# Cached keys turned by VectorE instead of TensorE, and stores of ScalarE's results issued from ScalarE's queue

## The chip, the cores and the metric

The kernel runs on one core of one Trainium2 chip. The core has a matrix engine (TensorE; PE in the profile, and PEld for its weight loads), three engines for elementwise work (VectorE = DVE, ScalarE = ACT, GpSimd = POOL), and SyncE (SP), which here does nothing but issue transfers. Sixteen transfer engines move data between the main memory and the on-chip memory. Each engine runs its own instructions in order; semaphores tell one engine that another has finished. The metric is the device time of one execution in microseconds, lower is better.

## What is computed

One step of a streaming encoder trunk for two groups of requests that share the weights: a prompt of 2048 tokens, and a sample of 8 sequences of 16 tokens, each with 1024 cached positions. All data is float32.

```python
h = rms_norm(x, norm_g[l])
(a_x, a_b, a_c, a_z, g_q, g_f, g_i, g_z,
 s_q, s_k, s_v, s_z, m_a, m_b, m_c) = split_cols(h @ w_in[l])
...
q = rms_norm(s_q.reshape(B, T, SB_HEADS, SB_DH), q_norm_g[l])
k = rms_norm(s_k.reshape(B, T, SB_HEADS, SB_DH), k_norm_g[l])
...
    k_all = jnp.concatenate([past_k.astype(k.dtype), k], axis=1)
    v_all = jnp.concatenate([past_v.astype(v.dtype), v], axis=1)
    o_sb = sb_attend(q, k_all, v_all, P + jnp.arange(T), jnp.arange(P + T))
o_c = o_sb.reshape(B, T, W_SB).astype(x.dtype) * jax.nn.silu(s_z)
...
m = jax.nn.sigmoid(m_a) * y_a + jax.nn.sigmoid(m_b) * y_b + jax.nn.sigmoid(m_c) * y_c
return x + m @ w_out[l], conv_new, S_new.astype(x.dtype), k, v
```

There are three branches: a gated convolution (A), a gated recurrence with a matrix state (B) and stick-breaking attention with 8 heads of 64 (C). In C the weight of a key is a sigmoid of its score times the product of one minus the sigmoids of all later keys. The sample's queries meet the 1024 cached keys of their sequence (`cache_k`, 8 x 1024 x 8 x 64 floats, 16.8 MB) besides their own; the prompt has no cache. New keys and values are outputs as well, and the three branch outputs are merged by sigmoid gates computed from `h`.

## The kernel before

Tokens go in 17 tiles of 128: tile 0 is the whole sample (8 x 16), tiles 1 to 16 are the prompt. Three groups of 5, 6 and 6 tiles (`GROUPS`) are projected one after the other. A float32 product is made of three products of rounded parts (`PASS3`), so each weight is kept as a high and a low half. `run_jobs` goes through a list of jobs for a group: `chan_job` gives 128 output columns for all tokens of a chunk (`proj_chan`, L710), `tok_job` 256 columns for one token tile at a time (`proj_tok`, L721). In the first group the weights are loaded, split and stored in that form; in the next two they are loaded again (`wload`, L208 and L201).

What is done with each projection's result:

- `gate_job` (24 jobs in each group, two chunks each): ScalarE takes the sigmoid from PSUM into `gm`, and a store to the scratch tensor `GM` follows (L1176, L1177).
- `post_v`: ScalarE copies the values into `vf`; two stores go to the output and to the scratch tensor `VV` (L835 to L837).
- `post_qk`: queries and keys are normed, turned on TensorE into a PSUM tile of its own and stored.

Each projection yields its cost after every few matmuls, and `run_jobs` spends it, times a rate, on background work kept as Python generators: the recurrence `hbg`, and in `bg` the sample's attention (from group 1) and the prompt's attention (from group 2 on). The costs that the generators yield are written out by hand. The order in which an engine gets its instructions is fixed when the kernel is built, from this order and from the dependences; on the chip an engine doesn't leave it.

`sample_attention` is the part in question. It goes over 8 sequences in three segments each, of 2, 3 and 3 blocks of 128 cached positions, last positions first, 24 segments and 64 blocks in all. For a segment:

- `keys(m)` loads each block, 128 positions x 512 columns, into `kc` with one transfer (L455; three buffers, shared under the tag `cst`), turns it with four TensorE transposes into a PSUM tile `tp` (L458) and copies that with ScalarE into the segment's `kt` (L459; two buffers), which has the head dimension on partitions and the position along the row. PSUM tiles `tp` have two buffers, shared with all other transposes of the kernel.
- `scores(m)` multiplies with the queries (L476), takes two sigmoids on ScalarE, and the running product on VectorE (L489, L490).
- `turned(m)` turns the weights on TensorE (L499) and loads the cached values; `values(m)` multiplies them (L522).

After a sequence's third segment, ScalarE copies the output of that sequence into `od` (L527), 128 partitions (8 heads x 16 queries) x 128 columns. Of these columns a head uses only one half. Eight stores of 16 x 64 put the halves in use to `OCS` (L529), [128 queries, 512]. At the end `OCS` is loaded in one transfer (L548), turned on TensorE (L551) and gated.

After the last group, the merge (L1440) and the output projection (L1471) follow, with the rest of the prompt's attention as background. All transfers but the indirect gathers of the recurrence are issued by SyncE.

Of the kernel before, what the change touches and what calls it, by code (L numbers as in the profile page):

```python
# [8 lines left out]
F32 = mybir.dt.float32  # L9
# [7 lines left out]
P = 128  # L17
# [3 lines left out]
NB = 8  # L21
TS = 16
# [76 lines left out]
def trunk(ctx: ExitStack, tc: tile.TileContext, x_prompt, x_sample, cache_conv, state_hgrn, cache_k, cache_v,  # L99
# [3 lines left out]
    nc = tc.nc  # L103
# [6 lines left out]
    def rows(prompt, sample, t):  # L110
        return sample if t == 0 else prompt[(t - 1) * P:t * P]
# [9 lines left out]
    vp_rows = v_prompt[0, 0].rearrange("t h d -> t (h d)")  # L121
    vs_rows = v_sample[0].rearrange("b t h d -> (b t) (h d)")
# [6 lines left out]
    dram = ctx.enter_context(tc.tile_pool(name="dram", bufs=1, space=DRAM))  # L129
# [11 lines left out]
    def ps_tp(dt=F32):  # L141
        return pst[0].tile([P, 512], dt, tag="tp", name="tp")

    def ps_pv():
        return ps.tile([P, 512], F32, tag="pv", name="pv", bufs=1)
# [8 lines left out]
    VV = dram.tile([NTOK, 8, 64], F32, name="VV")  # L154
# [1 line left out]
    OX = dram.tile([3, 4, 2, P, NTOK], F32R, name="OX")  # L156
    SZ = dram.tile([4, P, NTOK], F32, name="SZ")
    GM = dram.tile([3, 8, P, NTOK], F32, name="GM")
    OCS = dram.tile([P, 512], F32, name="OCS")


    idf = const.tile([P, P], F32, name="idf")
# [226 lines left out]
    def sample_attention():  # L389

        sx = ExitStack()
        sa = sx.enter_context(tc.tile_pool(name="sa", bufs=2, side="right"))
# [19 lines left out]
        for e in range(2):  # L412
            r = slice(64 * e, 64 * e + 64)
# [31 lines left out]
        def blocks(m):  # L445
            return 2 if order[m][1] == 2 else 3

        def keys(m):

            b, sg = order[m]  # L450
            kt = sa.tile([P, 4, 384], F32, tag="kt", name="kt", bufs=2)
            for bi in range(blocks(m)):
                blk = 3 * sg + bi
                kc = sa.tile([P, 512], F32, tag="cst", name="kc", bufs=3)
                nc.sync.dma_start(kc, cache_k[0, b, blk * P:(blk + 1) * P].rearrange("t h d -> t (h d)"))  # L455
                tp = ps_tp()
                for h in range(4):
                    nc.tensor.transpose(tp[:, h * P:(h + 1) * P], kc[:, h * P:(h + 1) * P], idf)  # L458
                nc.scalar.copy(kt[:, :, bi * P:(bi + 1) * P], tp.rearrange("p (h t) -> p h t", h=4))  # L459
                yield 1.3  # L460
            held[m] = [kt]

# [50 lines left out]
        def values(m):  # L513
            b, sg = order[m]
            at_, vs = held[m][2:4]
            if sg == 2:
                pvs[b] = ps_pv()
            pv = pvs[b]
            for bi, vc in enumerate(vs):
                for h in range(4):  # L520
                    c = bi * P + 32 * h
                    nc.tensor.matmul(pv[32 * h:32 * h + 32, 0:P].rearrange("p (e d) -> p e d", e=2),  # L522
                                     at_[:, c:c + 32], vc[:, 2 * h:2 * h + 2],
                                     start=sg == 2 and bi == 0, stop=sg == 0 and bi == 2, skip_group_check=True)
            if sg == 0:
                od = sa.tile([P, P], F32, tag="od", name="od", bufs=1)
                nc.scalar.copy(od, pv[:, 0:P])  # L527
                for h in range(8):
                    nc.sync.dma_start(OCS[b * TS:(b + 1) * TS, h * 64:(h + 1) * 64],  # L529
                                      od[h * TS:(h + 1) * TS, 64 * (h % 2):64 * (h % 2) + 64])  # L530


        last = len(order) - 1
        yield from keys(0)
        scores(0, masked(0))
        yield 0.7
        for m in range(last + 1):
            if m < last:
                yield from keys(m + 1)
            turned(m)  # L540
            yield 2.0
            z = masked(m + 1) if m < last else None
            values(m)
            if z is not None:
                scores(m + 1, z)
            yield 2.2
        oc = sa.tile([P, 512], F32, tag="cst", name="oc", bufs=3)
        nc.sync.dma_start(oc, OCS)  # L548
        tp = ps_tp()
        for j in range(4):  # L550
            nc.tensor.transpose(tp[:, j * P:(j + 1) * P], oc[:, j * P:(j + 1) * P], idf)  # L551
# [184 lines left out]
    def cols(chunk):  # L736
        return slice(chunk[0] * P, (chunk[-1] + 1) * P)
# [95 lines left out]
    def post_v(acc, t, s):  # L833
        vf = qk.tile([P, 256], F32, tag="kn", name="vf", bufs=5)
        nc.scalar.copy(vf, acc[:, :256])  # L835
        nc.sync.dma_start(rows(vp_rows, vs_rows, t)[:, s * 256:(s + 1) * 256], vf)
        nc.sync.dma_start(VV[t * P:(t + 1) * P, 4 * s:4 * s + 4].rearrange("t h d -> t (h d)"), vf)  # L837

# [298 lines left out]
    def group_jobs(g):  # L1139
        base = GROUPS[g][0][0] * P  # L1140
        chunks = GROUPS[g]
# [8 lines left out]
        def chan_job(name, blk, post, done=None):  # L1150
            def compute(w, ci, hT):
                acc = yield from proj_chan(w, hT)
                post(ci, acc)
                if done and ci == len(chunks) - 1:
                    done()
            return (chan_w(name, blk), compute, 1.0)
# [10 lines left out]
        for s in range(2):  # L1167
            qkv.append(tok_job("sv", s, post_v))
# [3 lines left out]
        def gate_job(x, d):  # L1172
            def post(ci, acc):
                n = len(chunks[ci]) * P
                gm = cv.tile([P, 384], F32, tag="gm", name="gm", bufs=3)
                nc.scalar.activation(gm[:, :n], acc[:, :n], AF.Sigmoid)  # L1176
                nc.sync.dma_start(GM[x, d][:, cols(chunks[ci])], gm[:, :n])  # L1177
            return chan_job(("ma", "mb", "mc")[x], d, post)

        def sz_job(j):  # L1180
# [192 lines left out]
    for g in range(len(GROUPS)):  # L1373
        run_jobs(g, group_jobs(g))
        if g == 0:
            p0.close()
            next(splitting)
            bg.add(sample_attention())
        if g == 1:
            prep.chunk(0)  # L1380
            bg.drain()
            for _ in splitting:
                pass
            mwx.close()
            p01.close()
            open_attention()
            for qi in range(4):
                bg.add(attention(qi), key=qi)
# [143 lines left out]
```

## Time and profile before

| | us |
|---|---|
| median of 3 runs (2876.0 to 2877.55) | 2877.0 |
| the profiled execution: its time | 2876.11 |
| its span, first to last instruction | 2873.2 |
| transfers | 649.76 MB, 370475 packets, mean 226 GB/s |

A profile is one execution as the hardware recorded it. Its page has the busy time of each engine, the chain of work that ended last (followed back from the last instruction, at each step to what released it), and groups of instructions that share line, engine, operation and tile, with count, busy time, mean duration, and the idle time of the engine in front of them with what ended it. In a row such as `tp<-idf,kc`, the written tile is on the left and the read ones on the right. A timeline row has start, duration, engine, line and operation; rows of one kind that follow each other are merged and counted. A transfer shows as the time its issue took on the issuing engine's queue (SPq for SyncE's), the time to landing, and the packets it was cut into; a packet is one contiguous run, and the share is the sum of the packets' times over 16 engines. Times of PE are modelled at their ends, as matmuls are pipelined, so its distances from start to start say more than its durations.

### The profile page before, as it was taken

What the parts mean: (1) busy time and instruction counts of PE and PEld (TensorE: products, weight loads), DVE (VectorE), ACT (ScalarE), POOL (GpSimd) and SP (SyncE); (2) the same over time, 40 slices, a digit from 0 to 9 for tenths busy, and PEclk for the clock granted to TensorE, in tenths of its full rate; (3) what the DMA queues carried; (4) which work ended last, traced back from release to release, by engine and by line L of the source; (5) the groups of instructions that cost most, each with busy time, mean ns of one, the idle gap of its engine ahead of it and who ended that gap; (6) DMA issues with size and microseconds to landing.
All of it is one profiled execution on the core that took longest, in us unless ns stands there. A gap on an engine that the chain in (4) does not pass through costs nothing.

```text
span 2873.2 us, 51723 instructions
## 1 busy us (share of the span) xinstructions
PE 2853.0 (99%) x19479; PEld 2662.3 (93%) x19479; DVE 1546.5 (54%) x3304; ACT 1018.7 (35%) x2375; POOL 331.8 (12%) x802
## 2 busy tenths in 40 slices
PE   9999999999999999999999999999999999999999
PEld 9999999999999999999999999999998888787888
DVE  5454635641344442545434747557485876867743
ACT  4333222242233332213334444434444444544420
POOL 3110000111200000001323111111010011010100
PEclk9999999999999999999999999999999999999999
DMA  8887777777678887746766454544447877878876
GB/s 306 305 276 247 231 241 244 231 243 243 212 249 266 276 265 243 243 167 192 237 215 202 146 173 136 173 139 151 144 145 238 286 234 239 266 250 266 271 250 210
DMA packets 370475, 649.76 MB, mean 226 GB/s; under 512 B 33481, under 2 KB 246306, under 8 KB 339506
## 3 DMA queue, kind: packets, MB, share of 16 engines
q1 hardware_dynamic: 369458, 644.36, 68.2%
q8 instruction: 154, 2.52, 0.4%
q0 software_dynamic: 768, 2.10, 0.2%
q14 instruction: 95, 0.78, 0.1%
HBM read 447.06 MB, written 199.27 MB: 225 GB/s over the span
## 4 chain that ended last, share of the span: by engine, by line
PE 76%; DVE 2%; DMA 2%; issue 1%; ACT 0%; POOL 0%; SPq 0%; DVEq 0%; POOLq 0%; ACTq 0%
PE acc L710 33%; PE acc L721 10%; PE acc L1440 9%; PE acc L1471 6%; PE pv L359 4%; PE tp L310 4%; PE z L330 2%; PE z L329 2%; PE z L1039 1%; PE tp L458 1%; DMA gate<-GM 1%; PE pv L522 1%; PE z L476 0%; PE hg L1086 0%; PE hg L826 0%
## 5 line engine op out<-in xcount | busy, mean ns | idle before, releaser
L710 PE MATMUL acc<-hx,w 128*128 128x384 f32 (+1 forms) x6816 | 1251.8, 333 | 0.1
L710 PEld LDWEIGHTS acc<-hx,w 128*128 128x128 f32 x6816 | 1106.5, 188 | 21.9 <-issue 15.2
L721 PE MATMUL acc<-w,hx 128*128 128x256 f32 x2544 | 328.6, 284 | 1.8 <-DVE hx L176 0.9
L342 DVE TENSOR_TENSOR_SCAN pr<-snb,carry 128x513 f32<-128x513 f32 x192 | 246.5, 1284 | 153.3 <-ACT snb L333 151.7
L721 PEld LDWEIGHTS acc<-w,hx 128*128 128x128 f32 x2544 | 310.9, 188 | 5.0 <-DVE hx L176 1.7
L311 ACT COPY aT<-tp 128x512 f32<-128x512 f32 (+2 forms) x320 | 167.6, 524 | 375.2 <-PE tp L310 361.3
L710 PE MATMUL acc<-hx,wst 128*128 128x384 f32 x1248 | 247.2, 344 | 0.0
L1440 PE MATMUL acc<-o,w 128*128 128x512 f32 (+2 forms) x1080 | 234.7, 363 | 1.8 <-DMA o<-OX 1.8
L333 ACT ACTIVATE snb<-z 128x512 f32<-128x512 f32 (+2 forms) x320 | 172.4, 539 | 144.5 <-PE z L330 140.4
L710 PEld LDWEIGHTS acc<-hx,wst 128*128 128x128 f32 x1248 | 215.4, 188 | 6.4 <-issue 3.7
L1440 PEld LDWEIGHTS acc<-o,w 128*128 128x128 f32 x1080 | 185.1, 188 | 33.8 <-issue 5.3
L347 DVE TENSOR_TENSOR sp<-sp,pr 128x512 f32<-128x512 f32 (+2 forms) x320 | 195.3, 611 | 29.2 <-POOL sp L338 3.7
L342 DVE TENSOR_TENSOR_SCAN pr<-snb,one 128x129 f32<-128x129 f32 (+3 forms) x128 | 114.4, 894 | 123.9 <-POOL snb L338 123.6
L310 PE MATMUL tp<-idf,sp 128*128 128x128 f32 x1088 | 171.3, 273 | 2.5 <-ACT aT L311 1.5
L335 ACT ACTIVATE sp<-z 128x512 f32<-128x512 f32 (+2 forms) x320 | 171.5, 536 | 0.0
L1471 PE MATMUL acc<-w,mh 128*128 128x256 f32 x816 | 161.2, 285 | 1.0 <-DVE yt L1479 0.8
L1176 ACT ACTIVATE gm<-acc 128x384 f32<-128x384 f32 (+1 forms) x144 | 68.2, 474 | 230.4 <-PE acc L710 197.5
L310 PEld LDWEIGHTS tp<-idf,sp 128*128 128x128 f32 x1088 | 131.8, 141 | 19.3 <-issue 4.4
L176 DVE TENSOR_TENSOR w<-wst,w 128x1024 fp32r<-128x1024 f32 x72 | 88.1, 1223 | 110.7 <-ACT w L175 107.9
L1471 PEld LDWEIGHTS acc<-w,mh 128*128 128x128 f32 x816 | 131.0, 188 | 7.2 <-issue 4.2
L329 PE MATMUL z<-Kt,Q 128*128 128x512 f32 (+2 forms) x320 | 128.8, 403 | 0.3 <-ACT sp L335 0.2
L359 PE MATMUL pv<-aT,Vt 128*64 128x512 f32 (+3 forms) x640 | 128.1, 535 | 0.0
(299 smaller groups left out, 3570.1 us busy)
## 6 DMA issues: line engine op xcount, KB each, us to landing
w<-W SPq DMA_DIRECT2D x168, 1024.0 KB, 6.0
W<-w SPq DMA_DIRECT2D x72, 1024.0 KB, 5.0
wst<-W SPq DMA_DIRECT2D x112, 512.0 KB, 5.1
wst<-in_w_in_dram SPq DMA_DIRECT2D x72, 512.0 KB, 5.1
GM<-gm SPq DMA_DIRECT2D x120, 192.0 KB, 3.7
W<-mwp SPq DMA_DIRECT2D x40, 512.0 KB, 4.2
Kt<-KT SPq DMA_DIRECT2D x160, 128.0 KB, 3.1
o<-OX SPq DMA_DIRECT2D x72, 256.0 KB, 4.7
```

The source lines that it names most:

```text
L310: nc.tensor.transpose(tp[:, j * P:(j + 1) * P], sp[:, j * P:(j + 1) * P], idf)
L311: nc.scalar.copy(aT[:, e, 0:nb, i * P:(i + 1) * P], tp[:, :w].rearrange("p (b q) -> p b q", q=P))
L329: nc.tensor.matmul(z[:, :w], Q1[:, i * P:(i + 1) * P], Kt[:, :w], start=True, stop=False)
L333: nc.scalar.activation(sn[:, 512 - w:512], z[:, :w], AF.Sigmoid, scale=-0.125)
L335: nc.scalar.activation(sp[:, :w], z[:, :w], AF.Sigmoid, scale=0.125)
L342: nc.vector.tensor_tensor_scan(pr[:, 512 - w:513][:, ::-1], s_in, s_in, one if diag else carry[e][i], ALU.mult, ALU.bypass)
L347: nc.vector.tensor_tensor(sp[:, :w], sp[:, :w], pr[:, 513 - w:513], ALU.mult)
L359: nc.tensor.matmul(pv[64 * e:64 * e + 64, c0:n], Vt[:, j, e], aT[:, e, j, c0:n], start=first and j == 0, stop=last and j == nb - 1, skip_g ...
L710: nc.tensor.matmul(acc[:, :n], w[0][a][:, k], hT[b][:, k, :n], start=k == 0 and i == 0, stop=k == KB - 1 and i == 2)
L721: nc.tensor.matmul(acc[:, :256], hT[b][:, k, ti * P:(ti + 1) * P], w[k // 4][a][:, k % 4], start=k == 0 and i == 0, stop=k == KB - 1 and i ...
L1440: nc.tensor.matmul(acc[:, :n], w[0][a][:, k, dd * P:(dd + 1) * P], box[x][b][:, k, sl], start=k == 0 and i == 0, stop=k == 3 and i == 2)
L1471: nc.tensor.matmul(acc[:, :256], box["l" if b else "h"][:, k, ti * P:(ti + 1) * P], w[k // 4][a][:, k % 4], start=k == 0 and i == 0, stop= ...
```

## The change

Three things change.

1. Cached keys. A block is loaded by four transfers of 32 partitions each. Partition 32a + p holds, for each of the four pairs of heads and each of the four groups of 32 positions, the 32 columns 32a to 32a + 31 of position p of that group. One VectorE instruction then turns all 32 x 32 squares of the tile and writes `kt`. The four TensorE transposes, the PSUM tile and ScalarE's copy are gone; the cost that `keys` yields is the same.
2. The sample's output. `od` is stored whole, with one transfer from ScalarE's queue in place of eight from SyncE's; at the end eight transfers from SyncE's queue, one for each head, pick the halves in use.
3. The stores of gates (`GM`) and values (the output and `VV`) are issued on ScalarE's queue in place of SyncE's. ScalarE wrote the tiles that they store.

```diff
-    OCS = dram.tile([P, 512], F32, name="OCS")
+
+    OCS = dram.tile([NB, P, 2, 64], F32, name="OCS")
...
             for bi in range(blocks(m)):
                 blk = 3 * sg + bi
-                kc = sa.tile([P, 512], F32, tag="cst", name="kc", bufs=3)
-                nc.sync.dma_start(kc, cache_k[0, b, blk * P:(blk + 1) * P].rearrange("t h d -> t (h d)"))
-                tp = ps_tp()
-                for h in range(4):
-                    nc.tensor.transpose(tp[:, h * P:(h + 1) * P], kc[:, h * P:(h + 1) * P], idf)
-                nc.scalar.copy(kt[:, :, bi * P:(bi + 1) * P], tp.rearrange("p (h t) -> p h t", h=4))
+
+                kc = sa.tile([P, 4, 4, 32], F32, tag="cst", name="kc", bufs=3)
+                keys_ = cache_k[0, b, blk * P:(blk + 1) * P].rearrange("(c p) h d -> p c (h d)", p=32)
+                keys_ = keys_.rearrange("p c (h x) -> p h c x", x=P)
+                for a in range(4):
+                    nc.sync.dma_start(kc[32 * a:32 * a + 32], keys_[:, :, :, 32 * a:32 * a + 32])
+                nc.vector.transpose(kt[:, :, bi * P:(bi + 1) * P].rearrange("p h (c q) -> p h c q", q=32), kc)
                 yield 1.3
...
                 nc.scalar.copy(od, pv[:, 0:P])
-                for h in range(8):
-                    nc.sync.dma_start(OCS[b * TS:(b + 1) * TS, h * 64:(h + 1) * 64],
-                                      od[h * TS:(h + 1) * TS, 64 * (h % 2):64 * (h % 2) + 64])
+                nc.scalar.dma_start(OCS[b].rearrange("r e d -> r (e d)"), od)
...
         oc = sa.tile([P, 512], F32, tag="cst", name="oc", bufs=3)
-        nc.sync.dma_start(oc, OCS)
+        for h in range(8):
+            nc.sync.dma_start(oc[:, h * 64:(h + 1) * 64], OCS[:, h * TS:(h + 1) * TS, h % 2])
...
         nc.scalar.copy(vf, acc[:, :256])
-        nc.sync.dma_start(rows(vp_rows, vs_rows, t)[:, s * 256:(s + 1) * 256], vf)
-        nc.sync.dma_start(VV[t * P:(t + 1) * P, 4 * s:4 * s + 4].rearrange("t h d -> t (h d)"), vf)
+        nc.scalar.dma_start(rows(vp_rows, vs_rows, t)[:, s * 256:(s + 1) * 256], vf)
+        nc.scalar.dma_start(VV[t * P:(t + 1) * P, 4 * s:4 * s + 4].rearrange("t h d -> t (h d)"), vf)
...
                 nc.scalar.activation(gm[:, :n], acc[:, :n], AF.Sigmoid)
-                nc.sync.dma_start(GM[x, d][:, cols(chunks[ci])], gm[:, :n])
+                nc.scalar.dma_start(GM[x, d][:, cols(chunks[ci])], gm[:, :n])
```

## Prediction

> **What bounds the kernel now.** I read the page's busy times and the chain that ended last, then the busy time by stage.
>
> ```profile
> span 2873.2 us, 51723 instructions
> ...
> PE 2853.0 (99%) x19479; PEld 2662.3 (93%) x19479; DVE 1546.5 (54%) x3304; ACT 1018.7 (35%) x2375; POOL 331.8 (12%) x802
> ...
> PE 76%; DVE 2%; DMA 2%; issue 1%; ACT 0%; POOL 0%; SPq 0%; DVEq 0%; POOLq 0%; ACTq 0%
> ```
>
> ```profile
> core 0: us, PE busy (x) PEld busy (x) DVE busy (x) ACT busy (x) POOL busy (x), PEclk, DMA share, GB/s
> 0.00:200.00 200.00, 195.84 (x1486) 192.94 (x1487) 91.86 (x189) 79.56 (x164) 45.11 (x104) 1.00 0.88 299
> 590.00:1140.00 550.00, 549.24 (x4304) 530.05 (x4304) 203.62 (x518) 175.49 (x439) 46.56 (x83) 1.00 0.76 249
> 1340.00:2170.00 830.00, 826.73 (x5372) 775.22 (x5371) 478.97 (x1039) 331.74 (x832) 148.72 (x345) 1.00 0.53 169
> ```
>
> TensorE sets the pace: of 2873.2 us it is idle for 20.2, and the chain runs through it. From 590 to 1140, where the cached keys are turned, it is idle for 0.76 us (550.00 less 549.24), VectorE is at 37%, ScalarE at 32%, the transfer engines at 0.76. So TensorE work taken away there is worth its full time, until the next thing is late. The first 200 us show the kernel with fuller transfer engines (0.88): TensorE then lost 4.16 us of 200.
>
> **The keys on TensorE (removed).** The groups of instructions by line, with count, busy us and mean ns:
>
> ```profile
> L458 PE MATMUL tp<-idf,kc 128*128 128x128 f32 x256 | 38.5, 273 | 0.8 <-DVE hx L176 0.8
> ...
> L459 ACT COPY kt<-tp 128x512 f32<-128x512 f32 x64 | 37.5, 588 | 58.6 <-PE tp L458 58.3
> ```
>
> The 273 ns of one transpose contain overlap with its neighbours, so I take the distance in the timeline (start, duration, engine and line):
>
> ```profile
> 930.50 0.49 ACT L1176 ACTIVATE gm<-acc 128x384 f32<-128x384 f32 x1 [1.53 <-PE acc L710]
> ...
> 931.02 0.32 SPq L1177 DMA_DIRECT2D GM<-gm  x1
> 931.43 2.40 SPq L455 DMA_DIRECT2D kc<-in_cache_k_dram  x3
> ...
> 944.14 0.54 PEld L458 LDWEIGHTS tp<-idf,kc 128*128 128x128 f32 x4
> ...
> 946.69 0.53 PEld L458 LDWEIGHTS tp<-idf,kc 128*128 128x128 f32 x4
> ...
> 947.18 3.11 PEld L710 LDWEIGHTS acc<-hx,w 128*128 128x128 f32 x18
> ...
> 950.28 0.53 PEld L458 LDWEIGHTS tp<-idf,kc 128*128 128x128 f32 x4
> ...
> 950.78 2.05 PEld L710 LDWEIGHTS acc<-hx,wst 128*128 128x128 f32 x12
> ```
>
> The four loads of a block begin at 946.69 and the next work at 947.18: 0.49 us, and 0.50 at 950.28. With 64 blocks (256 transposes by 4), 64 x 0.49 = 31.4 us leave TensorE. ScalarE loses 64 copies, 37.5 us, and the shared PSUM tiles `tp` are asked for 64 times less; neither is on the chain, so I count nothing for them.
>
> **The keys on VectorE (added).** No transpose runs on VectorE in this trace. Its nearest rows have the same 512 columns, a product of two tiles and a scan:
>
> ```profile
> L347 DVE TENSOR_TENSOR sp<-sp,pr 128x512 f32<-128x512 f32 x224 | 154.6, 690 | 20.8 <-POOL sp L338 2.6 <-DVE pr L342 0.5
> ...
> L342 DVE TENSOR_TENSOR_SCAN pr<-snb,carry 128x513 f32<-128x513 f32 x192 | 246.5, 1284 | 153.3 <-ACT snb L333 151.7
> ```
>
> I take the product's 0.69 us, since a transpose too is one pass: 64 x 0.69 = 44 us; with the scan's 1.284 it would be 82. All counted to this stage, VectorE goes from 204 us to about 248, or 286 of 550. That is covered by its own idle time, and I count 0. If the cover fails, the recurrence, which passes from VectorE to TensorE and back, waits behind a transpose, at most 1.284 us for a block; a tenth of that on the chain is 8 us, which belongs in the range. A gain is possible too, for the block no longer passes through PSUM and ScalarE.
>
> **The keys' loads (changed).** A block was one load of 128 rows of 2 KB. It becomes four loads that each read runs of 32 floats, 128 bytes: 16 runs in each of 128 rows, 2,048 packets for 128, in all 131,072 for 8,192. Three windows of the transfer view give the price of a packet (packets, MB, share of 16 engines). From 1165 to 1167, when little but the sample's small stores runs:
>
> ```profile
> q1 hardware_dynamic: 153, 0.02, 7.3%
> ```
>
> From 88.5 to 89.5, nearly all packets of 512 bytes:
>
> ```profile
> q1 hardware_dynamic: 589, 0.29, 96.6%
> ```
>
> From 590 to 1140, the stage itself:
>
> ```profile
> q1 hardware_dynamic: 73208, 135.33, 75.3%
> ```
>
> - 0.073 x 16 x 2 us / 153 = 15.3 ns at some 130 bytes.
> - 0.966 x 16 x 1 us / 589 = 26.2 ns at some 490 bytes.
> - 0.753 x 16 x 550 us / 73,208 = 90.5 ns at 1,849 bytes, 0.049 ns a byte.
>
> The old packets of 2,048 bytes took, by the third row, 100 ns: 8,192 of them, 51 us of all 16 engines. The new ones take 51 us if only bytes count (6.3 ns), 125 us at 15.3 ns, 215 us at 26.2 ns. I take 15.3, the row nearest in size. The stage's transfers, 0.753 x 550 = 414 us, become 414 - 51 + 125 = 488 us, in the 518 us that TensorE then needs: 94%. That is fuller than the first 200 us, where 4.16 us of 200 were lost, some of it to starting up; the same 2.1% of 518 us is 11 us. Against it stands how early the keys come:
>
> ```profile
> L455 SPq DMA_DIRECT2D kc<-in_cache_k_dram x64: 327/383/1494, 563.2 to 1119.0; - x64
> ...
> DMA to landing us min/median/max: 2.7/5.0/6.9
> ```
>
> Three were issued from 931.43 on and turned at 944.14, 946.69 and 950.28, over 12 us later, against at most 6.9 us to landing. So I count 5 us of new waits, between 0 and 11.
>
> The Trainium skill (DMA: Bandwidth & Descriptors, Specifications) asks for at least 512 bytes to reach line rate. In the rows above the bytes an engine moves in a ns fall from 18.8 (490 / 26.2) to 8.5 (130 / 15.3), so the trace agrees that small runs move less; whether one of 128 costs as much as one of 512 it doesn't show for loads.
>
> SyncE issues 192 loads of keys more. At 0.383 to 1.494 us that is 74 to 287 us, less the 64 stores of the sample's output and the gates and values below; it waits often enough to hold the former, and no matmul waits for it now, so 0.
>
> **The stores on ScalarE's queue (moved).** The issues by line (count, shortest, median and longest ns):
>
> ```profile
> L1177 SPq DMA_DIRECT2D GM<-gm x144: 319/320/1239, 112.0 to 2173.0; - x144
> ```
>
> ```profile
> L836 SPq DMA_DIRECT2D out_dram<-vf x34: 337/338/1092, 18.1 to 1470.9; - x34
> ```
>
> ```profile
> L837 SPq DMA_DIRECT2D VV<-vf x34: 332/430/1266, 18.5 to 1471.3; - x34
> ```
>
> ```profile
> SPq L1177 <- ACT gm L1176: 196.5, 94, 5.4
> ```
>
> 144 + 34 + 34 + 8 (the sample's output, one for eight) = 220 issues go to ScalarE. Each waits until its own result is written (gate done at 930.99, issued at 931.02: 0.03 us) and then issues for 0.32 us: 0.35 us during which all that is queued behind on ScalarE stands still: sigmoids of attention scores, copies of turned weights, other gates. 220 x 0.35 = 77 us, at worst 220 x 1.27 = 279 us, on an engine with 1,854 us of idle time. TensorE is idle 20.2 us beside 2,375 ScalarE instructions, 8.5 ns for each; for 220 more that is 1.9 us, and I count 2. SyncE no longer stands 196.5 us waiting for gates, so loads behind them can start sooner; as TensorE hardly waits for loads, that is 0 here, and a few us at best.
>
> **The sample's output at the end.** Before, eight small stores, one load, then the transposes:
>
> ```profile
> 1161.72 4.58 SPq L529 DMA_DIRECT2D OCS<-od  x8
> ...
> 1167.64 0.33 SPq L548 DMA_DIRECT2D oc<-OCS  x1
> ```
>
> ```profile
> L551 PE MATMUL tp<-idf,oc x4: 271/272/273, 1174.0 to 1174.3; 128*128 128x128 f32 x4
> ```
>
> After, one store, then eight loads: the 4.58 us of issues move from one side to the other. TensorE didn't wait there; 0, with 4.6 us once if it does.
>
> **The sum.** Against the profiled execution's 2876.11 us (span 2873.2 and 2.9 around it; 0.9 below the median of 2877.0, so the difference is applied to the median): -31.4 + 5 + 2 = -24.4, and 2877.0 - 24.4 = about 2852 us.
>
> **Rivals.**
> - *The transfer engines become the bound (slower).* If a run of 128 bytes holds an engine as long as one of 512, the stage needs 414 - 51 + 215 = 578 us of transfers, 28 more than its 550 now; with ScalarE's 2 us, 2907 us. It starts to decide when 363 us of other transfers and the keys exceed 518 us, at 18.9 ns a packet, and makes the kernel slower from 22.8 ns (550 us). For it: the stage is already at 0.76, and 15.3 ns comes from a mixture with very short packets, on stores. Against: a packet's price falls from 26.2 to 15.3 ns with its size, and the chance that the load side is flat below 512 is small. This is the skill's rule above taken at its word. Chance 0.17.
> - *ScalarE's stop becomes TensorE's (no change).* In the stage from 1340 to 2170 scores, transposes and gates all pass through ScalarE. The last token group, a third of all, has 48 gate stores and 24 of values; if each 0.35 us is seen in full by TensorE, 72 x 0.35 = 25 us come back, all of the 24 gained: 2877 us. For it: both PSUM buffers of scores are emptied by ScalarE alone. Against: ScalarE is only 40% busy there (331.74 of 830) and TensorE has projections between the scores. The Trainium skill (Perfetto Trace Analysis, DMA Instruction — HWDGE (DVE, Sync)) says that the issuing sequencers share one descriptor generator, by which a ScalarE store could stand behind SyncE's loads; no run so far shows two issuers at once. Chance 0.15, half-gains from late keys that end at the same place included.
> - *The time leaves the transposes but not TensorE:* it comes back as waiting for `kt`, up to the same 31.4 us, in front of the sample's scores. Those follow the keys only after the previous segment's transposes and values, and the keys land early, so only the 11 us above are left of it, in the range.
>
> **How the numbers follow.** A difference of 0.2%, 5.8 us, is about what a measurement of this kernel can tell from none. Forecast 0.68, all faster; no change 0.15 from the second rival; slower 0.17 from the first. The forecast's own range is 2843 (the whole 31.4 us and a few of freed queues) to 2866 (11 us for transfers and some of VectorE's 8). The range for 8 in 10 adds the second rival and the mild end of the first: 2843 to 2883.
>
> **What would show it.** In the profile after, TensorE should have 256 matmuls and 31 us less, and stay idle for less than 30 us. VectorE should have 64 transposes of 0.55 to 1.3 us. The queue of transfers should hold some 123,000 packets more, with the stage's share at 0.88 to 0.95. ScalarE's queue should carry 220 issues of 0.3 to 0.5 us. I am wrong if TensorE's idle time grows by over 20 us: in front of matmuls that wait for weights or keys, with the share near 1, it is the first rival; in front of scores, released by ScalarE, the second.

## The result and the profile after

The changed kernel takes 2996.0 us (median of 4 runs, 2992.0 to 2998.2) where the kernel before took 2876.5 in the same session: 1.0419 times as long, with a 95% interval of 1.0406 to 1.0432. It is 120 us slower, where 25 us faster was forecast. The profiled execution took 2994.26 us. From its page: span, busy times, the busy tenths of TensorE and its clock in 40 slices, packets, and the engines' shares of the chain that ended last.

```profile
span 2992.5 us, 51205 instructions
...
PE 2887.9 (97%) x19223; PEld 2660.0 (89%) x19223; DVE 1588.2 (53%) x3368; ACT 986.2 (33%) x2311; POOL 331.2 (11%) x802
...
PE   8999999999998887999999999999999999999999
...
PEclk9999999999998998999999999999999999999999
...
DMA packets 496474, 650.00 MB, mean 217 GB/s; under 512 B 166778, under 2 KB 380627, under 8 KB 465507
...
PE 86%; DMA 6%; DVE 3%; SPq 1%; ACT 1%; issue 1%; POOL 1%; ACTq 0%; DVEq 0%; POOLq 0%
```

TensorE has 256 matmuls fewer, as it should, and is yet busy for 35 us longer and idle for 104.6 us in place of 20.2. The slices with gaps, the 13th to the 16th, lie in one place: the second token group, in which the cached keys are turned. The first load of the third group's queries for the prompt's attention marks its end; it is issued at 1333.5 us before and at 1450.8 after. Up to the sample's first load of queries (551.1 before, 554.8 after) the two kernels agree within 4 us, and from the mark to the end within 2. So the stage holds all of the loss. By stage (columns as in the prediction's table: window, its length, busy times with counts, granted clock, share of the transfer engines, GB/s), first before:

```profile
560.00:1344.00 784.00, 778.61 (x5776) 755.46 (x5775) 321.06 (x868) 234.59 (x597) 61.30 (x114) 1.00 0.72 237
```

and the same stage after:

```profile
560.00:1463.00 903.00, 817.15 (x5554) 756.37 (x5553) 362.33 (x937) 202.73 (x538) 63.82 (x115) 0.95 0.70 208
```

The stage is 119 us longer. Idle time of TensorE went from 5.4 to 85.9 us (80.5 more). Its busy time grew by 38.5 us although 31.4 us of transposes were gone, so the work that stayed took some 70 us longer. The clock accounts for part of that: granted 0.95 of full speed, about 747 us of work take 39 us longer. (The trace grants it in stretches: half of full speed in 13 of them, of 3.4 to 10.2 us and 85 us together, and all of it between.) The rest, some 31 us, lies inside the matmuls' own busy time, which the trace does not split. And the transfer engines are less full than before (0.70 against 0.72), not fuller: the first rival is not what happened.

What TensorE waits for, in the stage (engine, line, releaser: us in total, times, longest):

```profile
PE z L478 <- DVE kt L461: 25.8, 9, 5.2
PE acc L711 <- DMA w<-W: 13.6, 8, 3.4
PE tp L501 <- DVE sps L492: 10.3, 8, 2.8
PE tp L1113 <- ACT on L1109: 10.1, 5, 2.6
```

Before, the longest of such waits was 1.4 us. Now the sample's scores wait for turned keys, the projections for weights. The view of the keys' tile says where the keys were (issues and transposes with shortest, median and longest ns; then what VectorE waited for, and who waited for the keys):

```profile
L460 SPq DMA_DIRECT2D kc<-in_cache_k_dram x256: 578/635/3199, 564.1 to 1254.7; - x128
L461 DVE STREAM_TRANSPOSE kt<-kc x64: 669/705/714, 578.7 to 1268.5; 128x512 f32<-128x512 f32 x64
...
  DMA kc<-in_cache_k_dram: 101.1, 17
...
  PE z L478: 25.8, 9
```

The transposes take what the prediction gave them. The issues don't: 256 of them at a median of 0.635 us are 163 us of SyncE's time, where 64 at 0.383 were 25 us. The durations themselves, added up over the trace, come to 193 and 31 us, because some issues last far longer than the median. They come in trains. SyncE's timeline (start, duration) around one of them:

```profile
979.98 10.18 SPq L460 DMA_DIRECT2D kc<-in_cache_k_dram  x12
990.20 0.65 SPq L209 DMA_DIRECT2D w<-W  x1
```

TensorE's timeline at the same place:

```profile
984.76 4.39 PE L711 MATMUL acc<-hx,w 128*128 128x384 f32 x24
994.30 1.51 PE L478 MATMUL z<-kt,qz 128*32 128x384 f32 x8 [5.15 <-DVE kt L461]
997.61 5.00 PE L711 MATMUL acc<-hx,w 128*128 128x384 f32 x17 [1.80 <-DMA w<-W]
```

A load of weights came next behind twelve loads of keys that took 10 us, and was issued at 990.20 without a wait of its own. TensorE stood first for the keys and then for these weights, and after the gap 17 matmuls took 5.00 us where 24 had taken 4.39. From 991.4 to 1001.5 the granted clock was half (the number in front of the share):

```profile
991.40:1001.50 10.10, 5.40 (x20) 4.15 (x21) 2.98 (x4) 1.50 (x3) 0.00 (x0) 0.50 0.98 320
```

SyncE's own waits from 560 to 1310 say the same for the stage. Before, it reached its loads of keys and of weights early and waited for their buffers:

```profile
SPq L455 <- PE tp L458: 52.9, 24, 7.5
SPq L208 <- PE acc L710: 45.1, 14, 10.3
```

After, it hardly does so; the buffers are mostly free by the time it comes to these loads:

```profile
SPq L460 <- DVE kt L461: 0.4, 1, 0.4
SPq L209 <- PE acc L711: 6.0, 3, 3.1
```

Once issued, the weights come as fast as before. From the issue to the end of the last packet it is 6.0 us in the median before (53 loads issued from 560 to 1270, at most 8.5) and 6.1 after (42 loads, at most 9.4), counted from the trace's packets of 8 KB in the order of their issue. So they are late by their issue, not on their way. This is the reading that the experiments had to confirm: SyncE's queue, at which the kernel's other loads stand too.

### The profile page after: what moved, and what is told of

Its sections match the earlier page's. It is cut to its first block, busy times and chain, and to the rows that moved or that the text cites. A ratio compares the mean times of both kernels' runs of the same rounds, so it can differ in the third digit from the quotient of the medians.

```text
span 2992.5 us, 51205 instructions
## 1 busy us (share of the span) xinstructions
PE 2887.9 (97%) x19223; PEld 2660.0 (89%) x19223; DVE 1588.2 (53%) x3368; ACT 986.2 (33%) x2311; POOL 331.2 (11%) x802
## 4 chain that ended last, share of the span: by engine, by line
PE 86%; DMA 6%; DVE 3%; SPq 1%; ACT 1%; issue 1%; POOL 1%; ACTq 0%; DVEq 0%; POOLq 0%
PE acc L711 42%; PE acc L722 11%; PE acc L1441 8%; PE acc L1472 6%; PE pv L360 4%; PE tp L311 4%; DMA w<-W 2%; PE z L331 2%; PE z L330 2%; PE z L1040 2%; DMA GM<-gm 1%; DMA gate<-GM 1%; SPq L460 1%; DMA xt<-in_x_prompt_dram 1%; PE pv L524 1%
## 5 line engine op out<-in xcount | busy, mean ns | idle before, releaser
L711 PEld LDWEIGHTS acc<-hx,w 128*128 128x128 f32 x6816 | 1122.1, 190 | 40.0 <-issue 23.1
L711 PEld LDWEIGHTS acc<-hx,wst 128*128 128x128 f32 x1248 | 222.4, 193 | 10.7 <-issue 5.7
```

What stands on the lines that cost most here:

```text
L711: nc.tensor.matmul(acc[:, :n], w[0][a][:, k], hT[b][:, k, :n], start=k == 0 and i == 0, stop=k == KB - 1 and i == 2)
```

## The experiments

Four theories were set against each other. **A**, the number of transfers: 256 loads in place of 64, in one queue. (In the program as built each transfer of SyncE or ScalarE signals on one of eight semaphores in turn, whichever of the two issues it, so it waits for the transfer eight places before it; this is so in both kernels. GpSimd's transfers have another eight.) **B**, the short packets: 2,048 in a block for 128, in the time that SyncE stands to issue them or in the transfer engines. **C**, the stores moved to ScalarE's queue, for which SyncE's loads now wait. **D**, turning on VectorE in itself. C is a relative of the prediction's second rival, D of its third. Ratios are to the kernel before on the same chip, with 95% intervals. Where a kernel below loads the keys into other places than the transposes need, it leaves out the right order of the keys; the amount of work stays the same.

### The parts by themselves

Keys as changed; all stores on SyncE as before (the sample's output stored whole):

```diff
-                nc.scalar.dma_start(OCS[b].rearrange("r e d -> r (e d)"), od)
+                nc.sync.dma_start(OCS[b].rearrange("r e d -> r (e d)"), od)
...
-                nc.scalar.dma_start(GM[x, d][:, cols(chunks[ci])], gm[:, :n])
+                nc.sync.dma_start(GM[x, d][:, cols(chunks[ci])], gm[:, :n])
```

and likewise the two stores of values.

> The changed kernel with all its stores back on SyncE's queue; keys as changed (four loads a block, VectorE). The sample's output stays one store and eight loads. Theory A, the number of transfers (every transfer waits for the one eight places before it, whichever queue issued that, so a block that takes four places instead of one delays the weights and values behind it): still slow, 2950 to 3000 us. Theory B, the short packets or the time to generate their descriptors: still slow, 2950 to 3000. Theory C, SyncE's transfers wait for ScalarE's stores with which they share nothing (the waits for the gates' stores in the trace after): most of the loss goes, 2850 to 2890.

Measured: 2976.7 us, ratio 1.0357 (1.034 to 1.0374). The other half, keys as before and the output, gates and values stored from ScalarE's queue, that is the second and third part of the change alone:

> The kernel before with the stores of gates, values and the sample's output on ScalarE's queue as changed; keys as before (one load a block, TensorE). Theory A: 56 small stores fewer, nothing else; 2865 to 2880 us. Theory B: the same. Theory C: 60 us or more slower, 2930 to 2990.

Measured: 2883.15 us, 1.0029 (1.0019 to 1.0038). So the keys carry 102 us of the loss and the stores' move 8 us by itself, 19 on top of the changed keys. In the profile after, SyncE's loads of keys do wait for ScalarE's stores:

```profile
SPq L460 <- DMA GM<-gm: 46.1, 12, 7.3
```

That wait is real and adds to the loss, but C is not the main cause: without it, 102 us remain.

### One load in place of four

One transfer brings a block with the same 2,048 packets of 128 bytes; VectorE writes the squares back interleaved:

```diff
...
-                for a in range(4):
-                    nc.sync.dma_start(kc[32 * a:32 * a + 32], keys_[:, :, :, 32 * a:32 * a + 32])
-                nc.vector.transpose(kt[:, :, bi * P:(bi + 1) * P].rearrange("p h (c q) -> p h c q", q=32), kc)
+                src = cache_k[0, b, blk * P:(blk + 1) * P].rearrange("(p c) h d -> p (c h d)", c=4)
+                src = src.rearrange("p (g a x) -> a p g x", a=4, x=32)
+                nc.sync.dma_start(kc.rearrange("p c h x -> p (c h) x"), src)
+                nc.vector.transpose(kt[:, :, bi * P:(bi + 1) * P].rearrange("p h (q c) -> p c h q", c=4), kc)
```

> The changed kernel with one load a block in place of four: partition 32a + p holds the columns 32a to 32a + 31 of positions 4p to 4p + 3, so the transfer has 128 partitions and the same 2048 packets of 128 bytes; VectorE turns the same squares and puts position 4q + c in its place with a stride of four. Theory A: the gain that was predicted comes, 2845 to 2870 us. Theory B: nothing changes, 2960 to 3000, or one issue takes over 2 us. Theory C: still slow, 2930 to 3000.

Measured: 3041.51 us, 1.0578 (1.0561 to 1.0596): slower than with four loads, and so against A as it was put. But the run brought something of its own. Issues, transposes, then SyncE's timeline, and the queue's packets (packets, MB, share of 16 engines) in a window of 6 us with little but keys:

```profile
L459 SPq DMA_DIRECT2D kc<-in_cache_k_dram x64: 559/608/9539, 563.4 to 1260.9; - x64
L460 DVE STREAM_TRANSPOSE kt<-kc x64: 1051/1087/1124, 571.4 to 1275.7; 128x512 f32<-128x512 f32 x64
```

```profile
909.63 14.40 SPq L459 DMA_DIRECT2D kc<-in_cache_k_dram  x3
```

```profile
q1 hardware_dynamic: 2468, 0.35, 35.1%
```

Three issues took 14.4 us, and only 411 packets moved in a us, with the 16 engines a third busy. Four loads at a time moved 762 in a us in the changed kernel (2 us of keys only, from 984):

```profile
q1 hardware_dynamic: 1524, 0.19, 60.5%
```

The source pattern of the single load has 4 as its slowest dimension. The Trainium skill (DMA: Bandwidth & Descriptors, Why a DMA increments its semaphore by 16 and not by 1) says that a transfer runs on the largest number of engines, up to 16, that divides the slowest dimensions of both sides: 4 here, 16 for a load of 32 partitions. The trace agrees. Beside its data a transfer leaves packets of 4 bytes: 4,224 for the 264 on ScalarE's queue in a run further below, 16 for each. On SyncE's queue this run (first row) has 768 fewer of them than the run with one load of whole rows (second row), so 12 fewer for each of the 64 loads: 459,938 - 337,826 = (131,072 - 8,192) - 768.

```profile
q1 hardware_dynamic: 459938, 608.43, 63.0%
...
q1 hardware_dynamic: 337826, 608.43, 65.1%
```

So this run tells little of A or B, and two others with the same pattern share the fault. One has the kernel before, turned on TensorE, with one load of 128-byte packets:

```diff
-                nc.sync.dma_start(kc, cache_k[0, b, blk * P:(blk + 1) * P].rearrange("t h d -> t (h d)"))
+                src = cache_k[0, b, blk * P:(blk + 1) * P].rearrange("(p c) h d -> p (c h d)", c=4)
+                src = src.rearrange("p (g a x) -> a p g x", a=4, x=32)
+                nc.sync.dma_start(kc.rearrange("p (g x) -> p g x", x=32), src)
```

> The kernel before, with each block of keys loaded by one transfer of 2048 packets of 128 bytes (partition 32a + p gets the columns of quarter a); TensorE turns the tile as before, all stores on SyncE's queue. The tile's contents are rearranged, so the sample's attention has the right amount of work on the wrong keys. Theory B: the loss is all in the packets, so slower than the kernel with one load and VectorE's turning by about the 31 us that TensorE's transposes take, less the 8 of the queue: 3030 to 3080 us. Theory A (number of transfers): as before, 2870 to 2885. Theory D: 2870 to 2900.

Measured: 3049.57 us, 1.0608 (1.059 to 1.0626). The other has one load with packets of 512 bytes, turned on VectorE (against the first run of this part):

```diff
-                src = src.rearrange("p (g a x) -> a p g x", a=4, x=32)
-                nc.sync.dma_start(kc.rearrange("p c h x -> p (c h) x"), src)
+                src = src.rearrange("p (c a y) -> a p c y", a=4, y=P)
+                nc.sync.dma_start(kc.rearrange("p c h x -> p c (h x)"), src)
```

> The changed kernel with one load a block in runs of 128 columns: 512 packets of 512 bytes in place of 2048 of 128, turned by VectorE. A quadrant of partitions then holds one pair of heads, and scores still multiply as if it held a quarter of each, so the sample's attention has the right amount of work on the wrong keys. Theory B: a quarter of the descriptors, 64 x 512 at 1.3 to 2.4 ns are 43 to 79 us of handing out in place of 173 to 315, which SyncE's idle time holds: 2850 to 2885 us. A theory by which any rearranging load is slow: 2950 or more.

Measured: 2947.82 us, 1.0258 (1.0241 to 1.0275). With a quarter as many packets the loss is smaller, which points to B, but with 4 engines in use neither settles it.

### Number against size, with all 16 engines

Four loads of 32 whole rows each, packets of 2 KB, in the kernel before:

```diff
-                nc.sync.dma_start(kc, cache_k[0, b, blk * P:(blk + 1) * P].rearrange("t h d -> t (h d)"))
+                rows_ = cache_k[0, b, blk * P:(blk + 1) * P].rearrange("t h d -> t (h d)")
+                for a in range(4):
+                    nc.sync.dma_start(kc[32 * a:32 * a + 32], rows_[32 * a:32 * a + 32])
```

> The kernel before, with each block of keys loaded by four transfers of 32 whole rows (2 KB packets) instead of one of 128; TensorE turns them as before, all stores on SyncE's queue. Theory A: slower by 60 us or more, 2940 to 3000 us. Theory B: SyncE issues 192 transfers more, the packets are the old ones; 2875 to 2885. Theory C: 2875 to 2885.

Measured: 2922.0 us, 1.0162 (1.0145 to 1.0179): 47 us for nothing but three issues more for each block.

```profile
L457 SPq DMA_DIRECT2D kc<-in_cache_k_dram x256: 310/420/2099, 562.2 to 1185.2; - x128
```

The same with packets of 128 bytes, four loads, still turned on TensorE:

```diff
-                nc.sync.dma_start(kc, cache_k[0, b, blk * P:(blk + 1) * P].rearrange("t h d -> t (h d)"))
+                keys_ = cache_k[0, b, blk * P:(blk + 1) * P].rearrange("(c p) h d -> p c (h d)", p=32)
+                keys_ = keys_.rearrange("p c (h x) -> p h c x", x=P)
+                for a in range(4):
+                    nc.sync.dma_start(kc[32 * a:32 * a + 32].rearrange("p (h c x) -> p h c x", h=4, c=4),
+                                      keys_[:, :, :, 32 * a:32 * a + 32])
```

> The kernel before, whose blocks of cached keys come in four loads of 32 partitions each with packets of 128 B (as in the changed kernel), and which TensorE still turns; the stores stay on SyncE. Packets of 128 B put the keys' squares in other places, so the scores are of rearranged keys. If the number of transfers is what costs (A), this is the run with four loads of whole rows again: 2915 to 2930 us. If in addition the many short packets make SyncE stand longer at each load (B), it loses what the changed keys alone lost and the 31 us of TensorE's transposes on top, less a few for VectorE: 2990 to 3015 us, with an issue of about 0.63 us in the middle and trains of several us, against 0.31 to 0.42 with whole rows.

Measured: 3002.13 us, 1.0443 (1.0426 to 1.0461), 80 us above the four loads of rows. The issues, and the wait of the projections:

```profile
L458 SPq DMA_DIRECT2D kc<-in_cache_k_dram x256: 579/635/2939, 562.8 to 1263.1; - x128
```

```profile
PE acc L714 <- DMA w<-W: 18.0, 7, 4.5
```

Nothing of the change but the loads is in this kernel, no VectorE turning and no store on ScalarE, and it loses as much as the changed kernel. A and B both count, and B more.

### Turning on VectorE with the old load

One load of whole rows for a block, VectorE turns, stores on ScalarE:

```diff
...
-                for a in range(4):
-                    nc.sync.dma_start(kc[32 * a:32 * a + 32], keys_[:, :, :, 32 * a:32 * a + 32])
+                nc.sync.dma_start(kc.rearrange("p h c x -> p (h c x)"),
+                                  cache_k[0, b, blk * P:(blk + 1) * P].rearrange("t h d -> t (h d)"))
```

> The changed kernel with each block of keys loaded as before, one transfer of 128 rows of 2 KB, and turned by VectorE square by square all the same; the squares are then not in their places, so the sample's attention has the right amount of work on the wrong keys. Stores on ScalarE's queue as changed. Theory B (short packets: their descriptors are handed out at 1.3 to 2.4 ns each, and SyncE stands meanwhile): the predicted gain less the 8 us that the queue alone cost, 2845 to 2865 us. Theory D (the turning on VectorE itself delays the recurrence or the scores): 2885 us or more.

Measured: 2858.34 us, 0.9946 (0.9929 to 0.9962). Against the run with the stores alone (2883.15) the turning on VectorE gains 24.8 us. D falls, and the gain that was forecast is there when the loads stay as they were. The keys' rows, and the stage from 590 to 1140:

```profile
L457 SPq DMA_DIRECT2D kc<-in_cache_k_dram x64: 327/374/1573, 563.9 to 1069.5; - x64
L459 DVE STREAM_TRANSPOSE kt<-kc x64: 669/702/714, 568.1 to 1094.0; 128x512 f32<-128x512 f32 x64
```

```profile
590.00:1140.00 550.00, 546.62 (x4210) 526.87 (x4209) 251.14 (x623) 148.07 (x394) 49.15 (x88) 0.99 0.78 256
```

Then the same kernel with four loads of 32 rows for each block:

```diff
-                nc.sync.dma_start(kc.rearrange("p h c x -> p (h c x)"),
-                                  cache_k[0, b, blk * P:(blk + 1) * P].rearrange("t h d -> t (h d)"))
+                rows_ = cache_k[0, b, blk * P:(blk + 1) * P].rearrange("t h d -> t (h d)")
+                for a in range(4):
+                    nc.sync.dma_start(kc[32 * a:32 * a + 32].rearrange("p h c x -> p (h c x)"),
+                                      rows_[32 * a:32 * a + 32])
```

> The changed kernel in everything but the form of the packets: a block of keys comes in four loads of 32 whole rows (packets of 2 KB), and VectorE turns it; the squares lie in other places, so the scores are of rearranged keys. One load a block gave 2858 us, and four loads of whole rows cost 47 us when TensorE turned the keys. If the costs add up, 2895 to 2910 us, and the rest to the changed kernel's 2996 us, about 90 us, is that of the short packets (B). If the loss needs both VectorE's turning and four transfers, whatever their packets (A with three buffers of keys as the limit), it comes near 2970 us or more.

Measured: 2889.16 us, 1.0048 (1.0031 to 1.0065).

```profile
L459 SPq DMA_DIRECT2D kc<-in_cache_k_dram x256: 310/420/1536, 565.0 to 1149.6; - x128
```

From here to the changed kernel only the form of the packets is left. That gives the ladder, one edit at a time (medians; the kernel before, run beside each, took 2874.8 to 2876.5):

| step | us | difference |
|---|---|---|
| before | 2874.8 | |
| stores on ScalarE's queue | 2883.15 | +8.4 |
| keys turned on VectorE, one load of rows | 2858.34 | -24.8 |
| four loads of 32 rows | 2889.16 | +30.8 |
| packets of 128 bytes (the changed kernel) | 2996.02 | +106.9 |

### The same loads from another queue

The changed kernel with the loads of keys issued by GpSimd:

```diff
-                    nc.sync.dma_start(kc[32 * a:32 * a + 32], keys_[:, :, :, 32 * a:32 * a + 32])
+                    nc.gpsimd.dma_start(kc[32 * a:32 * a + 32], keys_[:, :, :, 32 * a:32 * a + 32])
```

> The changed kernel with the four loads of each block issued by GpSimd in place of SyncE; all else as changed. If the loss is that SyncE stands over the short packets with weights and values queued behind: 2850 to 2900 us. If the engines themselves are slowed by short packets, whoever issues them, or GpSimd makes descriptors no faster (64 blocks in over 700 us): 2950 us or more, with TensorE waiting for kt.

Measured: 2875.93 us, 1.001 (0.9998 to 1.0022): the whole loss is gone. But GpSimd's transfers don't have the same packets (issues, then the queue that holds them):

```profile
L460 POOL DMA_DIRECT2D kc<-in_cache_k_dram x256: 684/797/1516, 563.3 to 1103.2; - x128
```

```profile
q0 software_dynamic: 8960, 18.89, 2.9%
```

Of the 8,960 packets 768 with 2.10 MB were there before; the 8,192 new ones have 16.8 MB. By the sizes in the trace 4,096 of them are of 4 KB and 4,096 of 4 bytes, so a packet of this queue holds 32 of the runs of 128 bytes, and is not one contiguous run. Nor do GpSimd's transfers take turns on the eight semaphores of SyncE. So this run takes away the short packets and the shared semaphores together with SyncE's standing. ScalarE's transfers keep both, so its run tells them from SyncE's standing (loads of keys on ScalarE, gates and values on SyncE):

```diff
-                    nc.sync.dma_start(kc[32 * a:32 * a + 32], keys_[:, :, :, 32 * a:32 * a + 32])
+                    nc.scalar.dma_start(kc[32 * a:32 * a + 32], keys_[:, :, :, 32 * a:32 * a + 32])
...
-                nc.scalar.dma_start(GM[x, d][:, cols(chunks[ci])], gm[:, :n])
+                nc.sync.dma_start(GM[x, d][:, cols(chunks[ci])], gm[:, :n])
```

> The changed kernel, with the 256 loads of keys, short packets and all, issued by ScalarE, and gates and values stored by SyncE as before. The run tells apart two readings of what short packets cost (B). If they cost because SyncE stands for 0.64 us to several us at each load while loads of weights are queued behind, the loss goes with the queue: 2865 to 2920 us, ScalarE standing some 190 us in the stage instead, and SyncE's waits short. If they cost in the transfer engines or in what hands out descriptors to all queues, the weights come late just the same: 2960 us or more, and TensorE waits for w. If ScalarE's standing stops the scores, TensorE waits for ScalarE's tiles instead (the prediction's second rival, with longer stops).

Measured: 2889.07 us, 1.0048 (1.0032 to 1.0064), against 2976.7 with the same loads on SyncE. The issues, ScalarE's queue, and what TensorE waited for most:

```profile
L460 ACTq DMA_DIRECT2D kc<-in_cache_k_dram x256: 585/587/4835, 560.2 to 1143.8; - x128
```

```profile
q10 hardware_dynamic: 136320, 17.32, 4.0%
```

```profile
PE acc L711 <- ACT gm L1177: 3.9, 3, 2.0
PE acc L711 <- DVE hgz L1137: 3.6, 2, 1.9
PE z L478 <- DVE kt L461: 3.5, 3, 1.2
```

The short packets are all there, 131,072 of the 136,320 in q10, and no matmul of the stage is listed as waiting for weights. SyncE again comes early to the loads of weights, and waits for their buffers (560 to 1310):

```profile
SPq L209 <- PE acc L711: 58.2, 20, 10.3
```

VectorE waits for keys almost as long as in the changed kernel (101.1 us), which here stops TensorE for 3.5 us:

```profile
  DMA kc<-in_cache_k_dram: 96.5, 26
```

So the larger part of the loss follows the queue at which the loads of weights stand, not the packets, VectorE's wait for keys or the shared semaphores, all of which this run keeps. What ScalarE pays shows in its timeline; it stands too. A copy of values comes 4.72 us after the copy ahead of it; the row names the matmul as releaser, but two loads of keys stood on ScalarE until 712.34, 0.04 us before it starts:

```profile
708.12 4.22 ACTq L460 DMA_DIRECT2D kc<-in_cache_k_dram  x2
712.38 0.37 ACT L836 COPY vf<-acc 128x256 f32<-128x256 f32 x1 [4.72 <-PE acc L722]
```

Finally the same kernel with the loads issued by GpSimd, and gates and values still stored by SyncE:

```diff
-                    nc.scalar.dma_start(kc[32 * a:32 * a + 32], keys_[:, :, :, 32 * a:32 * a + 32])
+                    nc.gpsimd.dma_start(kc[32 * a:32 * a + 32], keys_[:, :, :, 32 * a:32 * a + 32])
```

> The changed kernel, whose loads of keys GpSimd issues, and whose gates and values SyncE stores, as in the kernel before; the sample's output stays on ScalarE. With the loads on GpSimd and those stores on ScalarE it took 2876 us, and the stores' move alone cost 8 us in the kernel before. If the move of the stores costs the same here, 2865 to 2871 us, faster than the kernel before. If the 8 us came from stores that SyncE's loads wait for through the shared places in flight, whichever queue issues them, no change: 2873 to 2878 us.

Measured: 2869.19 us, 0.9983 (0.9973 to 0.9992), the shortest time of a kernel that computes all of the reference: 127 us less than the changed kernel, and 0.17% less than the one before, an interval that just leaves 1 out. Of the 24.8 us that VectorE can save, some 6 remain. The stage from 590 to 1140 shows GpSimd's price, 222 us of its time for 47 before, and TensorE idle for 11 us:

```profile
590.00:1140.00 550.00, 538.79 (x4114) 517.09 (x4116) 243.94 (x602) 142.59 (x379) 222.44 (x323) 0.99 0.86 252
```

## Why the prediction was wrong

**The step that failed** is what ends the part on the keys' loads: "SyncE issues 192 loads of keys more. At 0.383 to 1.494 us that is 74 to 287 us ... it waits often enough to hold the former, and no matmul waits for it now, so 0." The bounds of the issue time held (0.635 us in the middle, and 163 us more in all, 193.3 less 30.6), but the cover did not. That SyncE waits often in the kernel before does not mean that its instructions may come later: it waits for buffers, and issues the next load of weights the moment one is free. "No matmul waits for it now" says that the loads come in time with the queue as it was, not by how much they may slip. The term set at 0 measured +30.8 us for the number of loads and +106.9 for their form, and the run from ScalarE's queue shows that most of it is the queue. It should have stood among the rivals, with its place: loads of weights behind trains of loads of keys. In the sum's own terms, up to 163 us more of issues in a stage of 784, on the queue that feeds the bounding engine, was a slower case. That this is near the loss is no proof of the size, though: four loads of rows add 92 us of issues (123 in all) and cost 31.

**The transposes on TensorE, -31.4:** right. The count fell by 256, and with the old load the turning on VectorE gained 24.8 us in all.

**VectorE, 0.69 us each, covered:** right, 0.705 measured, and nothing lost where the loads were left as they were.

**The price of a packet, 15.3 ns:** a little high. 0.605 x 16 x 2 us / 1,524 = 12.7 ns in the window of keys shown above. In the trace's own durations a packet of 128 bytes took 13 ns in the median, one of 512 took 27, and one of 2 KB 84, not 100. That is far from the 18.9 ns at which the first rival begins, and a packet of 128 bytes is not as dear as one of 512. The share of 0.88 to 0.95 that followed from it did not come, since the work was not offered fast enough: 0.70.

**The keys come early, 5 us of waits:** wrong, and by the same step. The 12 us of lead were a property of a queue with 64 issues; VectorE now waited 101.1 us for keys, and TensorE 25.8 us for VectorE.

**ScalarE's issues, 2 us:** the size was off. The issue of a gate took what was said, at most 0.393 us; a store of values to `VV` took up to 1.400:

```profile
L1178 ACTq DMA_DIRECT2D GM<-gm x144: 326/326/393, 116.2 to 2292.1; - x144
```

```profile
L838 ACTq DMA_DIRECT2D VV<-vf x34: 326/456/1400, 18.5 to 1590.0; - x34
```

The move cost 8.4 us by itself, between the 2 counted and the 25 of the second rival. In the profile of that run TensorE is idle for 27.3 us in place of 20.2, and waits for one of ScalarE's tiles for 4.2 us, where it was 0.2 before:

```profile
PE acc L722 <- ACT hx L176: 4.2, 3, 2.4
```

That is the mechanism that was named, for a part of the 8.4; no run splits the rest.

The first of these rows also answers the point drawn from the Trainium skill on one descriptor generator for all issuing sequencers: 47 of the 144 issues of gates overlap one of SyncE, whose loads of keys took up to 3.199 us, and none took longer than 0.393. For them the rule does not show here. The long issues to `VV` come with one of SyncE beside them (up to 1.400 us) and without (up to 1.271).

**What was to prove it wrong** named the sign (TensorE idle over 20 us longer, in front of matmuls that wait for weights or keys) but tied it to a share near 1. The third case, an idle TensorE and transfer engines that are not full, meant here that the transfers were issued late. The Trainium skill (Perfetto Trace Analysis, What "DMA-bound" means) lists as the second way of being bound that the issuing engine's track is solid with issues. SyncE's was not solid: its issues fill 352 of the 710 us from 560 to 1270 after, and 222 of the 584 from 560 to 1144 before. What stood behind a train was late all the same.

**What stays open.** From four loads of rows to four of short packets SyncE's issues of keys grow from 123 to 193 us, by 70, and the time by 107. The trace shows contributions to the difference (issues of up to 3.2 us, the clock at 0.95, waits for ScalarE's stores), but no run splits them. What makes some issues last several us is not shown either. In the single load's train 6,144 packets were issued in 14.40 us, 427 a us, where 411 a us moved, so its issues may have been held to the pace of the transfers; no run tells whether they were.

## What to carry over

Before adding transfers to a queue, add up its issues in the stage and look at what stands behind them: a queue that feeds the bounding engine has no free time merely because its engine is often waiting. When TensorE idles and the transfer engines are not full, look for the issuer; one run with the same loads, in the same packets, issued by another engine tells issue from transfer. Count an operation's whole path when it is moved to another engine: the loads that VectorE's layout needed cost 137.7 us here, and taking the work off TensorE gave 24.8.

## What the hardware showed beside that

- An issue does not grow in step with its packets: shortest times of 0.310 us (32 packets of 2 KB), 0.327 (128 of 2 KB), 0.578 (512 of 128 bytes) and 0.559 (2,048 of 128 bytes, on 4 engines by the count above). The longest, in the same order, are 2.1, 1.6, 3.2 and 9.5 us.
- One load with a slowest dimension of 4 moved 411 packets in a us, nearly all of 128 bytes, where four loads of 32 partitions moved 762.
- GpSimd's queue carried runs of 128 bytes in packets of 4 KB, 32 runs in each.
- VectorE's transpose of 128 x 512 took 0.705 us; written back with a stride (the single load's runs) it took 1.087.
- The granted clock, 1.00 in the stage before, was 0.95 once TensorE idled in short pieces for a tenth of it: half speed in 13 stretches of 3.4 to 10.2 us.
